# RWKV time mixing: 22 instead of 18 units transposed by the DMA crossbar, the last two loads held so that loads and transposes take turns, slot shifts by ScalarE

## Chip, cores, metric

One core of a Trainium2 chip. The metric is device time of one execution in microseconds (us). Executions of one kernel mostly agree within some tenths; an execution counts as slow when it is over 1.5% above the fastest of its kernel, and comparisons use fast runs. Kernels sent together ran on one chip, beside fresh runs of the kernel before.

## The reference

```python
x_prev[:, 1:, :] = x[:, :-1, :]                    # x: 16 x 2048 x 256, float32
xv = x * time_mix_v + x_prev * (1 - time_mix_v)    # and xr alike
v = xv @ value_weight                              # 256 x 256
r = xr @ receptance_weight
out = (sigmoid(r) * v) @ output_weight             # the k branch isn't used
```

## The kernel before

The 16 batches are cut into 64 units of 512 rows. Each unit needs x transposed (features on partitions). Then, per unit: `psum_r` (4 matmuls), sigmoid on ScalarE, `psum_v` (4), their product `z_sb` on VectorE, `psum_o` (8), its copy on ScalarE, and a store per two units. The mixing with x_prev is a scaled copy of `xt` (VectorE, GpSimd, ScalarE by turns) plus an add of `xt` one slot further on (VectorE).

The first 46 units are transposed by TensorE, six units ahead, and copied out of PSUM by ScalarE; the last 18 by the DMA crossbar (a DMA that transposes what it moves), issued by the sync queue (SP):

```python
BYDMA = 4 * UB + 2                  # UB = 4 units a batch; 18 units by the crossbar
CROSS = NU - BYDMA - LOOK           # 64 - 18 - 6 = 40: first unit in which TensorE transposes nothing
...
xpool  = tile_pool(name="xpool", bufs=6)     # loaded batches, bf16
xtpool = tile_pool(name="xtpool", bufs=3)    # transposed batches
...
def load(b):                        # float32 in DRAM to bf16: a casting load, so from GpSimd's queue
    return nc.gpsimd.dma_start(out=x_bf[b], in_=rows(b), max_dma_last_dim=8192)

def by_dma(b, lo, hi, after=None):
    op = nc.sync.dma_start_transpose(out=xt[b][:, 1 + lo : 1 + hi]..., in_=x_bf[b][:, lo:hi]...)
    if after is not None:
        tc.add_manual_dep(op.ins, after.ins.name, SYNC, reason="not beside a load")
...
for g in range(NU - 1):
    project(ps_r, g, 0); sigmoid
    if g == CROSS:
        by_dma(B - 5, 1 * UJ, 3 * UJ, last_load)       # half of batch 11, after load 15
    advance(...)                                       # TensorE transposes; load b + 5 at each batch
    for b in range(B - 4, B):                          # batches 12 to 15, whole
        if g == max(UB * (b - 2) - 1, CROSS + 1):
            new_xt(b); by_dma(b, 0, J); shifted = b
    output(g - 2) ...; scale, add, project(ps_v, g, 1), z_sb, scale_pool, add ...
    if shifted is not None and g == max(UB * (shifted - 2), CROSS + 2):
        nc.sync.dma_start(out=xt[shifted][:, 0, :, 1:P], in_=xt[shifted][:, J, :, 0 : P - 1])
```

Each queue works in program order. So SP's queue carries stores, crossbar transposes and slot shifts one behind the other, and GpSimd's carries its products and the loads.

## Time and profile before

| | kernel before |
|---|---|
| time, median of 5 | 204.13 us (203.94 to 207.01) |
| span of the profiled run | 202.7 us |
| psum_r start to psum_r start, TensorE transposing / not | 3.05 / 2.60 us |
| last load lands | 134.3 us |

The interval between two psum_r starts, read off the timeline unit by unit, is the measure: whatever exceeds 2.60 us in the crossbar stage is a stall. The prediction below shows the views. Two lines that it quotes only in prose are needed later. They are the DMA queues in 117 to 127 us of the kernel before (packets, MB, share of 16 engines): loads, then stores.

```profile
q0 software_dynamic: 302, 1.17, 57.8%
q1 hardware_dynamic: 246, 1.88, 46.4%
```

The loads took 5.78 of 10 us for 1.17 MB, so 5.2 us of all engines for one batch (1024 KB as bf16, which the view counts as 1.05 MB); the stores 4.64 us for 1.88 MB, so 2.6 us for a store of two units (1024 KB). The share adds up the times of packets and can pass 1.

### The profile page before, as it was taken

How to read it: one execution, taken by the hardware profiler on the slowest of the kernel's cores; microseconds unless marked ns; L12 is line 12 of the kernel's file. 1: busy time of each engine (PE TensorE's matmuls, PEld its weight loads, DVE VectorE, ACT ScalarE, POOL GpSimd, SP SyncE). 2: the span in 40 equal slices, each digit the busy share in tenths (PEclk: the TensorE clock that was granted, in tenths of full speed). 3: DMA queues.
4: the chain of work that ended last, by engine and by line, in shares of the span. 5: the costliest groups of instructions: out<-in, count | busy, mean ns of one | idle time of the engine just before them, and what ended most of it. 6: DMA issues, size and time to landing. Idle time of an engine off the chain costs nothing.

```text
span 202.7 us, 3923 instructions
## 1 busy us (share of the span) xinstructions
PE 195.4 (96%) x1436; PEld 126.2 (62%) x1436; DVE 187.6 (93%) x301; ACT 179.3 (88%) x198; POOL 83.7 (41%) x109
## 2 busy tenths in 40 slices
PE   8899999999999999999999999999899999999992
PEld 7565676666666666666666666655455566665570
DVE  3799999999999999999999999999999999999952
ACT  2599899999999999999999999998798999999981
POOL 1655443462542545344363542443444444444200
PEclk9999999999999999999999999999999999999999
DMA  5999999999999999999999999999999999899475
GB/s 164 294 159 215 241 276 274 279 282 272 293 318 309 313 318 302 293 308 303 289 301 289 293 309 308 292 308 197 287 174 376 246 352 244 276 409 372 200 304 207
DMA packets 32186, 57.00 MB, mean 281 GB/s; under 512 B 20772, under 2 KB 22056, under 8 KB 29096
## 3 DMA queue, kind: packets, MB, share of 16 engines
q1 hardware_dynamic: 27216, 40.50, 59.3%
q0 software_dynamic: 4800, 16.12, 40.1%
q8 instruction: 11, 0.18, 0.3%
q10 hardware_dynamic: 152, 0.13, 0.2%
q14 instruction: 7, 0.06, 0.1%
HBM read 34.34 MB, written 33.55 MB: 335 GB/s over the span
## 4 chain that ended last, share of the span: by engine, by line
PE 80%; DVE 7%; ACT 5%; issue 4%; DMA 2%; SPq 0%; DVEq 0%; ACTq 0%
PE psum_v L279 24%; PE psum_r L279 22%; PE psum_o L303 22%; PE ps_t L200 9%; DVE z_sb L548 3%; DMA w_f<-n_receptance_weight_dram 2%; ACT s_sb L513 2%; DVE mix L271 2%; ACT o_sb L335 2%; DVE mix L249 1%; PE psum_r L293 1%; PE ps_t L303 1%; ACT mix L491 1%; ACT xt L216 0%; PE ps_t L279 0%
## 5 line engine op out<-in xcount | busy, mean ns | idle before, releaser
L259 POOL TENSOR_SCALAR mix<-xt,c_sb 128x1024 bf16<-128x1024 bf16 (+1 forms) x55 | 61.4, 1116 | 92.3 <-DVE mix L271 80.8
L548 DVE TENSOR_TENSOR z_sb<-s_sb,psum_v 128x1024 bf16<-128x1024 bf16 x63 | 76.6, 1215 | 3.4 <-PE psum_v L279 1.7
L271 DVE TENSOR_TENSOR mix<-mix,xt 128x1024 bf16<-128x1024 bf16 x112 | 77.4, 699 | 1.7
L279 PEld LDWEIGHTS <-w_bf 128*128 128x128 bf16 x516 | 48.6, 98 | 39.5 <-issue 2.1
L513 ACT ACTIVATE s_sb<-psum_r 128x1024 bf16<-128x1024 f32 x63 | 65.0, 1032 | 6.2 <-PE psum_r L279 5.9
L335 ACT COPY o_sb<-psum_o 128x1024 f32<-128x1024 f32 x60 | 61.1, 1018 | 7.0 <-PE psum_o L303 7.0
L279 PE MATMUL psum_v<-mix,w_bf 128*128 128x512 bf16 (+1 forms) x256 | 65.3, 377 | 1.2 <-DVE z_sb L548 1.1
L279 PE MATMUL psum_r<-mix,w_bf 128*128 128x512 bf16 (+1 forms) x252 | 64.2, 377 | 0.3 <-ACT s_sb L513 0.3
L303 PE MATMUL psum_o<-wo_bf,z_sb 128*128 128x256 bf16 x494 | 64.4, 273 | 0.1
L303 PEld LDWEIGHTS <-z_sb 128*128 128x128 bf16 x512 | 49.9, 98 | 20.1 <-DVE z_sb L364 0.8
L216 ACT COPY xt<-ps_t 128x1024 bf16<-128x1024 bf16 x38 | 38.7, 1029 | 0.0
L200 PEld LDWEIGHTS <-x_bf 128*128 128x128 bf16 x344 | 22.4, 98 | 9.5 <-DMA x_bf<-in_x_dram 0.5
L200 PE MATMUL ps_t<-ident,x_bf 128*128 128x128 bf16 x344 | 25.7, 219 | 0.0
L249 DVE TENSOR_SCALAR mix<-xt,c_sb 128x1024 bf16<-128x1024 bf16 (+1 forms) x50 | 23.4, 475 | 0.0
L491 ACT ACTIVATE mix<-xt,c_sb 128x1024 bf16<-128x1024 bf16 x11 | 12.8, 1160 | 0.0
L109 POOL DMA_DIRECT2D x_bf<-in_x_dram x14 | 10.5, 752 | 0.0
L271 DVE TENSOR_TENSOR mix<-mix,xt_first 128x1024 bf16<-128x1024 bf16 x15 | 10.1, 681 | 0.1
L259 POOL TENSOR_SCALAR mix<-xt_first,c_sb 128x512 bf16<-128x512 bf16 x6 | 4.2, 694 | 8.0 <-DVE xt_first L408 8.0
L249 DVE TENSOR_SCALAR mix<-xt_first,c_sb 128x512 bf16<-128x512 bf16 x22 | 6.7, 351 | 0.2
L216 ACT COPY xt_first<-ps_t 128x1024 bf16<-128x1024 bf16 x5 | 5.2, 1035 | 0.0
L144 PE MATMUL ps_t<-zeros 128*128 128x128 bf16 x31 | 3.1, 282 | 1.0 <-DVE zeros L87 1.0
L209 ACT CAST xt_first<-ps_t 128x512 bf16<-128x512 f32 x4 | 2.1, 588 | 1.6 <-PE ps_t L200 1.6
(63 smaller groups left out, 46.9 us busy)
## 6 DMA issues: line engine op xcount, KB each, us to landing
out_dram<-o_sb SPq DMA_DIRECT2D x28, 1024.0 KB, 9.7
x_bf<-in_x_dram POOLq DMA_DIRECT2D x14, 1024.0 KB, 27.6
out_dram<-o_sb SPq DMA_DIRECT2D x4, 512.0 KB, 3.6
out_dram<-o_sb SPq DMA_DIRECT2D x6, 256.0 KB, 2.1
x_bf<-in_x_dram POOLq DMA_DIRECT2D x5, 256.0 KB, 6.9
o_sb<-in_x_dram SPq DMA_DIRECT2D x2, 512.0 KB, 5.3
o_sb<-in_x_dram SPq DMA_DIRECT2D x2, 256.0 KB, 2.9
out_dram<-o_sb SPq DMA_DIRECT2D x3, 128.0 KB, 2.0
```

The lines of the kernel that those rows point to most:

```text
L109: return nc.gpsimd.dma_start(out=x_bf[b], in_=rows(b), max_dma_last_dim=8192)
L200: nc.tensor.transpose(out=ps[:, jj], in_=src[:, jj, ko * P : (ko + 1) * P], identity=idn)
L216: nc.scalar.copy(out=xt[b][:, j0 : j0 + UJ], in_=ps)
L249: nc.vector.tensor_scalar(out=mixed(piece)[:, :, ko], in0=xt[b][:, slots(piece), ko], scalar1=c_sb[:, m, ko : ko + 1], scalar2=None, op0=A ...
L259: op = nc.gpsimd.tensor_scalar(out=mixed(piece)[:, :, 1], in0=xt[b][:, slots(piece), 1], scalar1=c_sb[:, m, 1:2], scalar2=1.0, op0=ALU.mul ...
L271: return nc.vector.tensor_tensor(out=mixed(piece), in0=mixed(piece), in1=xt[b][:, slots(piece, 1)], op=ALU.add)
L279: nc.tensor.matmul(out=ps[:, mo, :], lhsT=w_bf[:, m, ko, mo * P : (mo + 1) * P], rhs=mixed((b, m, e * TU + lo, e * TU + hi))[:, :, ko], st ...
L303: nc.tensor.matmul(out=ps[:, slot, :], lhsT=z[:, ko, jj * P : (jj + 1) * P], rhs=wo_bf[:, ko, :], start=(ko == 0), stop=(ko == KO - 1),)
L335: nc.scalar.copy(out=o_sb[b][:, j0 : j0 + UJ, :], in_=ps)
L491: nc.scalar.activation(out=mixed(piece)[:, :, ko], in_=xt[b][:, slots(piece), ko], func=ACT.Copy, scale=c_sb[:, m, ko : ko + 1],)
L513: nc.scalar.activation(out=s_sb, in_=ps_r, func=ACT.Sigmoid)
L548: nc.vector.tensor_tensor(out=z_sb, in0=s_sb, in1=ps_v, op=ALU.mult)
```

## The change

Intent: four more units without TensorE transposes and ScalarE evictions. As these begin while loads are still due, loads 14 and 15 are held: load 14 waits for the transpose of batch 11, the transposes of batch 12 wait for load 14, and so on. The slot shift becomes a small ScalarE copy.

```diff
-    BYDMA = 4 * UB + 2
+    BYDMA = 5 * UB + 2
     CROSS = NU - BYDMA - LOOK                        # now 36
+    CROSS_AT = {B - 6: CROSS - 2, B - 5: CROSS - 1, B - 4: CROSS + 4, B - 3: CROSS + 6, B - 2: CROSS + 12, B - 1: CROSS + 15}
+    HELD_AT = {B - 2: CROSS, B - 1: CROSS + 8}
+    AFTER = {B - 6: B - 3, B - 4: B - 2, B - 2: B - 1}
...  # in advance()
-                last_load = load(b + 5)
+                if b + 5 not in HELD_AT:
+                    loads[b + 5] = load(b + 5)
...  # in the loop over units
+        for b, at in CROSS_AT.items():
+            if g == at:
+                ...
+                crossed = by_dma(b, lo, hi, loads[AFTER[b]] if b in AFTER else None)
+            if g == UB * (b - 1) and b > B - 6:
+                nc.scalar.copy(out=xt[b][:, 0, :, 1:P], in_=xt[b][:, J, :, 0 : P - 1])
...  # at the end of a unit
-        if shifted is not None and ...:
-            nc.sync.dma_start(...)
+        for b, at in HELD_AT.items():
+            if g == at:
+                loads[b] = load(b)
+                tc.add_manual_dep(loads[b].ins, crossed.ins.name, SYNC, reason="not beside a transpose")
```

More of the change, by code (lines that the diff above doesn't have):

```diff
@@ L186, in by_dma @@
             tc.add_manual_dep(op.ins, after.ins.name, SYNC, reason="not beside a load")
+        return op
     def transposes(i):
@@ L412 @@
     tnext = 1
-    last_load = None
+    loads = {}
+    crossed = None
     def advance(limit):
-        nonlocal tnext, last_load
+        nonlocal tnext
         while tnext <= min(limit, NU - 1):
@@ L498 @@
     z_prev2 = z_prev = None
-    shifted = None
     for g in range(NU - 1):
@@ L513 @@
         nc.scalar.activation(out=s_sb, in_=ps_r, func=ACT.Sigmoid)
-        if g == CROSS:
-            by_dma(B - 5, 1 * UJ, 3 * UJ, last_load)
         advance(START_T[g] if g < len(START_T) else g + LOOK)
-        for b in range(B - 4, B):
-            if g == max(UB * (b - 2) - 1, CROSS + 1):
-                new_xt(b)
-                by_dma(b, 0, J)
-                shifted = b
+        for b, at in CROSS_AT.items():
+            if g == at:
+                whole = b > B - 6
+                if whole:
+                    new_xt(b)
+                lo, hi = (0, J) if whole else (UJ, 3 * UJ)
+                crossed = by_dma(b, lo, hi, loads[AFTER[b]] if b in AFTER else None)
+            if g == UB * (b - 1) and b > B - 6:
+                nc.scalar.copy(out=xt[b][:, 0, :, 1:P], in_=xt[b][:, J, :, 0 : P - 1])
         if LATE_O < g < NU - 2:
@@ L556 @@
             advance(4)
-        if shifted is not None and g == max(UB * (shifted - 2), CROSS + 2):
-            nc.sync.dma_start(
-                out=xt[shifted][:, 0, :, 1:P], in_=xt[shifted][:, J, :, 0 : P - 1]
-            )
+        for b, at in HELD_AT.items():
+            if g == at:
+                loads[b] = load(b)
+                tc.add_manual_dep(loads[b].ins, crossed.ins.name, SYNC, reason="not beside a transpose")
         z_prev2, z_prev = z_prev, z_sb
```

## The prediction

> **What bounds the kernel now.** I read first the busy shares, then the groups, then the busy time by stretch, then the timeline and the sync queue's waits around the place that the change edits (130 to 180 us), last the DMA queues there. The page gives the roles:
>
> ```profile
> PE 195.4 (96%) x1436; PEld 126.2 (62%) x1436; DVE 187.6 (93%) x301; ACT 179.3 (88%) x198; POOL 83.7 (41%) x109
> L216 ACT COPY xt<-ps_t 128x1024 bf16<-128x1024 bf16 x38 | 38.7, 1029 | 0.0
> L200 PE MATMUL ps_t<-ident,x_bf 128*128 128x128 bf16 x344 | 25.7, 219 | 0.0
> ```
>
> TensorE is the bound (96%), and 344 of its matmuls only transpose. The busy time by stretch shows two regimes. The columns after the stretch and its length are the engines' busy us with counts, then granted clock, DMA share and GB/s:
>
> ```profile
> 80.00:100.00 20.00, 20.00 (x158) 13.23 (x156) 18.93 (x27) 18.58 (x21) 8.79 (x9) 1.00 1.04 300
> 140.00:150.00 10.00, 9.36 (x57) 5.37 (x56) 10.00 (x13) 8.42 (x9) 4.32 (x6) 1.00 1.10 216
> 150.00:160.00 10.00, 9.79 (x62) 5.74 (x60) 10.00 (x14) 9.09 (x10) 4.46 (x5) 1.00 1.10 327
> 160.00:170.00 10.00, 10.00 (x63) 6.05 (x62) 9.97 (x15) 9.18 (x11) 4.52 (x5) 1.00 1.05 302
> ```
>
> With transposes on TensorE a unit takes 3.05 us (in the timeline psum_r starts at 123.85 and 126.90); without them 2.60 us (157.24, 159.84, 162.44). In the second regime VectorE is full too: 9.97 of 10 us. So from there a delay of VectorE is a delay of the kernel. The DMA share is about 1 in all four rows, the second point to keep. Counting psum_r starts back from the end (unit 63 at 194.78), unit 40 starts at 132.99; the crossbar starts there:
>
> ```profile
> 139.40 1.46 POOL L259 TENSOR_SCALAR mix<-xt,c_sb 128x1024 bf16<-128x1024 bf16 x1 [2.93 <-DVE z_sb L548]
> 139.79 1.35 DVE L249 TENSOR_SCALAR mix<-xt,c_sb 128x1024 bf16<-128x1024 bf16 x1
> 142.92 1.02 PE L279 MATMUL psum_v<-mix,w_bf 128*128 128x512 bf16 x4 [0.64 <-DVE z_sb L548]
> 150.38 1.21 DVE L271 TENSOR_TENSOR mix<-mix,xt 128x1024 bf16<-128x1024 bf16 x1
> ```
>
> The first transposes, issued at 134.44, land 4.8 us later, at 139.2; GpSimd's product at 139.40 waited for them, ran beside VectorE's product (1.35 us in place of 0.48) and TensorE lost time. Between psum_r starts, units 43, 46 and 47 take 3.40, 2.67 and 2.99 us in place of 2.60: **1.26 us of stalls** in the whole late part.
>
> **The DMA side.** A load's time from issue to landing, for the loads issued at 91.07, 103.25 and 115.44 (batches 13, 14, 15), each from the DMA view of a window on that issue:
>
> ```profile
> x_bf<-in_x_dram POOLq DMA_DIRECT2D x1, 1024.0 KB, 26.1
> x_bf<-in_x_dram POOLq DMA_DIRECT2D x1, 1024.0 KB, 22.5
> x_bf<-in_x_dram POOLq DMA_DIRECT2D x1, 1024.0 KB, 18.9
> ```
>
> So they land at 117.2, 125.8 and 134.3, one per 8.6 us, though one is issued per 12.2: a queue works itself off until 134. The sync queue then works in order:
>
> ```profile
> SPq L181 <- DMA x_bf<-in_x_dram: 2.8, 1, 2.8
> SPq L558 <- DMA xt<-x_bf: 5.8, 4, 2.1
> 165.79 8.15 SPq L181 DMA_TRANSPOSE xt<-x_bf  x1
> ```
>
> A whole batch's transpose holds this queue 5.1 to 8.2 us and lands 7.3 to 10.1 us after its issue; the two at 155.01 and 165.79, with stores just ahead of them, took 9.1 and 10.1.
>
> **What the Trainium skill says.** (1) "DMA: Bandwidth & Descriptors", "Anatomy of one DMA — SWDGE (gpsimd) path": a semaphore wait for a DMA is served by the issuing sequencer before dispatch. The trace agrees: the sync queue itself stood 2.8 us for the last load. (2) The same page, "Latency and other measured facts", gives 261 GB/s for one non-contiguous DMA transpose and about 350-400 for contiguous. The trace is slower: 217 GB/s where only a transpose moves, 1 MB in 4.8 us. (3) The same page, "Issuing engines are not separate DMA queues": all queues share the 16 engines. In 117 to 127 us the load queue took 57.8% of them and the sync queue 46.4%: full. (4) "SBUF — State Buffer", "Who interferes with whom": a VectorE operation with two SBUF inputs, or in a two-port mode, excludes a GpSimd operation that reads SBUF. The trace agrees: 0.68 us adds take 1.21 at 150.38, beside GpSimd at 149.94.
>
> **The change, part by part.** Here CROSS goes from 40 to 36 and units 42 to 45 leave TensorE.
>
> *Removed.* 4 units of transposes: 4 x (3.05 - 2.60) = **-1.8 us** on the path. ScalarE loses four 1.03 us evictions, beside TensorE, free. If the first crossbar data come well ahead of their use, the 1.26 us of stalls go as well. Best case: -3.06, 204.13 to 201.1 us.
>
> *Added on ScalarE.* Five slot copies of 128x254. The trace has 0.37 us for a 128x256 ScalarE copy. ScalarE waits 0.41 us in each pair of late units, but the PSUM buffers turn over with only about 0.2 to 0.3 us to spare, so I charge 0.06 each: **+0.3 us**, if the data have landed. They replace four DMAs of 2.8 to 4.6 us.
>
> *Moved: the held loads.* Load 14 is issued at the end of unit 36 by GpSimd's queue and waits for batch 11's transpose; load 15 at the end of unit 44 and waits for batch 13's. That GpSimd must stand and wait is the step I trust most. Without stalls psum_r would start at about 123.0 (unit 37), 125.6 (38), then every 2.6.
> - Batch 10's half waits for load 13 at 117.2, keeps the sync queue 2.9 us, lands near 122; its first use is unit 37's GpSimd product (3.1 us after psum_r, 126.1): in time.
> - A store, then batch 11's transpose at 120.9, landing some 8.2 us later: 129. GpSimd should have begun unit 37's product at 126.1; it begins after the wait and 0.75 us of issue, near 129.8, and is done at 131. VectorE wants it after unit 38's z, at about 129.8: 1.2 us, and then the next product runs beside an add. **+1.5 us.**
> - Load 14 shares the engines with two stores, so it lands near 138 (the alone rate, 1 MB in 4.8 us at 218 GB/s early on, plus 4.8 us of two stores at 437 GB/s). Batch 12's transpose stands before it in the sync queue, lands 145; ScalarE's copy in unit 44 wants it at about 144.8: **+0.5.**
> - Batch 13, behind a store: about 152. Load 15 goes then. GpSimd's product of unit 45 is wanted near 149 and comes near 153.3: VectorE loses **+2.0.**
> - Load 15 lands near 162, batch 14's transpose at 169.5; ScalarE's copy in unit 52 wants it near 167.5: **+1.5.** Batch 15 (177) is about in time.
>
> Sum with my middle durations: -3.06 + 0.3 + 5.5 = +2.7, 206.9 us. With 1 us less in each of the seven DMA steps, the stalls nearly go, except 1 us: 202.4.
>
> **The rivals.** *A: the turns fit.* 201.1 to 202.5. For it: the offsets (+4, +6, +8, +12, +15) look chosen from a trace; a load takes 8.6 us, four units 10.4; and no load then halves a transpose's rate. Against it: unit 36 is only one unit after the transposes that its load awaits. *B: the chain load, transpose, transpose, load, transpose becomes the bound,* through GpSimd's and ScalarE's waits, 204 to 208.5. For it: the DMA is full from start to unit 56 already, and the change adds 4 units, some 5 us of engine time at 4.8 us a batch; VectorE has no slack to make a stall good. *C: nothing of the gain but no chain,* the first stall alone (1.5 to 2.5): 202.5 to 204. I give A 0.3, B 0.5, C 0.2.
>
> **Range and chances.** The middle of these is **205.0 us**; A's good end gives the low limit 201.3, B's bad end, with a chain 1.5 us longer, the high one 208.6. Faster by over 2% needs 200.1, under the best case: 0.03. Slower by over 2% needs 208.2: 0.15. Within 2%: 0.82.
>
> **What would show it.** Right: 312 transposing matmuls instead of 344; 2.60 us units from unit 36; GpSimd's queue waiting for a transpose at the two held loads, 3 to 5 us each; VectorE's adds waiting for GpSimd after it; ScalarE waiting in a slot copy. Wrong: batch 11 landing before 126, load 14 under 7 us from issue, or GpSimd busy as before at units 37 and 45; then A holds. The sum fails downwards if DMA steps run faster alone than I took from the shared ones, and upwards if the waits also hold back stores until ScalarE finds no output buffer.

## The result

| | before | after |
|---|---|---|
| median of 5 | 204.13 us | 217.69 us (215.37 to 219.17) |
| fast runs | | 215.37, 216.02, 217.69 |
| ratio of fast runs | | 1.0601 (1.0548 to 1.0654) |
| profiled span, mean granted clock | 202.7 us, 1.00 | 217.2 us, 0.968 (a slow run) |

Ratios here are the mean time of one kernel's fast runs over that of the other's of the same rounds, so not quite the ratio of the medians. The change is 6% slower; 217.69 lies outside 201.3 to 208.6. The profile of the changed kernel fell in a slow execution; its fast runs are 1.2 to 3.6 us shorter than it. What follows rests on events that fast profiles of its variants repeat.

The page of the changed kernel, its busy shares and its transposing matmuls:

```profile
PE 200.4 (92%) x1404; PEld 126.6 (58%) x1404; DVE 187.6 (86%) x298; ACT 179.8 (83%) x201; POOL 83.0 (38%) x109
L204 PE MATMUL ps_t<-ident,x_bf 128*128 128x128 bf16 x312 | 23.3, 219 | 0.0
```

Work went out as planned (312 instead of 344) and the span grew all the same: VectorE has the same 187.6 us in 86% of the span. So it is waiting. Where, the busy time by stretch tells (columns as in the prediction; 0.83 and 0.70 are the granted TensorE clock):

```profile
130.00:140.00 10.00, 7.36 (x37) 3.88 (x35) 6.81 (x9) 5.87 (x7) 5.25 (x6) 0.83 0.97 244
...
150.00:160.00 10.00, 7.29 (x44) 4.19 (x43) 6.12 (x9) 8.68 (x10) 2.76 (x4) 1.00 1.07 320
160.00:170.00 10.00, 8.78 (x45) 5.05 (x46) 8.63 (x11) 6.13 (x7) 4.01 (x5) 0.83 1.02 260
170.00:180.00 10.00, 6.93 (x41) 3.82 (x39) 8.12 (x12) 6.00 (x8) 3.40 (x4) 0.96 0.77 179
180.00:190.00 10.00, 9.66 (x44) 5.22 (x44) 5.76 (x8) 7.46 (x9) 2.23 (x2) 0.70 1.10 311
```

Until 121 us both kernels run alike. From unit 36 the 2.60 us units come as intended, then four stalls (psum_r interval beyond 2.60, both units where two follow on each other): units 39 and 40: 4.3 us; unit 45: 1.75; units 47 and 48: 4.5; units 53 and 54: 6.4. With some tenths elsewhere, 17.6 us. Against that stand 1.8 us of gain and the 1.26 us of old stalls, gone: 17.6 - 3.06 = 14.5, which is the difference of the two spans, 217.2 - 202.7.

The chain behind the stalls is plain in the sync queue's timeline (start, length, what) and in the landing times of the two held loads, issued at 130.22 and 157.60:

```profile
120.66 7.34 SPq L184 DMA_TRANSPOSE xt<-x_bf  x1
...
142.37 4.82 SPq L184 DMA_TRANSPOSE xt<-x_bf  x1
...
147.99 7.06 SPq L184 DMA_TRANSPOSE xt<-x_bf  x1
...
172.26 4.83 SPq L184 DMA_TRANSPOSE xt<-x_bf  x1
```

```profile
x_bf<-in_x_dram POOLq DMA_DIRECT2D x1, 1024.0 KB, 12.0
x_bf<-in_x_dram POOLq DMA_DIRECT2D x1, 1024.0 KB, 14.5
```

Batch 11's transpose starts at 120.66; load 14 goes out at 130.22 and lands at 142.2; batch 12 follows at 142.37, batch 13 at 147.99 (landing 9.1 us later); load 15 at 157.60 to 172.1; batch 14 at 172.26, landing at 179. The timeline of the other engines at the first held load, and at ScalarE's two waiting slot copies:

```profile
130.22 0.75 POOL L112 DMA_DIRECT2D x_bf<-in_x_dram  x1 [5.75 <-DVE z_sb L555]
...
131.02 2.21 POOL L263 TENSOR_SCALAR mix<-xt,c_sb 128x1024 bf16<-128x1024 bf16 x2
132.18 2.20 DVE L275 TENSOR_TENSOR mix<-mix,xt 128x1024 bf16<-128x1024 bf16 x2 [2.13 <-POOL mix L263]
133.84 1.04 PE L283 MATMUL psum_r<-mix,w_bf 128*128 128x512 bf16 x4 [2.64 <-DVE mix L275]
...
136.24 1.91 PE L283 MATMUL psum_v<-mix,w_bf 128*128 128x512 bf16 x4
```

```profile
149.71 0.40 ACT L528 COPY xt<-xt 128x254 bf16<-128x254 bf16 x1 [1.54 <-DMA xt<-x_bf]
...
178.97 0.40 ACT L528 COPY xt<-xt 128x254 bf16<-128x254 bf16 x1 [3.58 <-DMA xt<-x_bf]
```

GpSimd stands 5.75 us before the load. (The engine named as releaser, VectorE's z_sb, had long been done; the load waits for the transpose.) VectorE then waits 2.13 us for GpSimd and TensorE 2.64 us for VectorE. And one thing was not foreseen: four matmuls that took 1.03 us now take 1.91. The granted clock is read from short stretches of the busy-time view:

```profile
131.30:134.70 3.40, 0.86 (x4) 0.40 (x5) 2.52 (x3) 0.38 (x1) 2.08 (x3) 1.00 0.85 154
134.70:138.10 3.40, 3.40 (x14) 1.86 (x13) 2.50 (x4) 2.93 (x4) 1.82 (x3) 0.53 1.04 235
138.10:141.50 3.40, 3.40 (x21) 1.85 (x20) 2.93 (x4) 2.37 (x3) 0.96 (x2) 0.97 0.92 283
```

After 3.4 us in which TensorE worked only 0.86, its clock is halved for the next 3.4, and 14 matmuls pass where 21 do afterwards. The same happens at 162.0 to 165.4 and, for twice as long, at 179.1 to 185.9. The length of the wait doesn't decide it alone. In a fast run of a variant below ("A load with the DMA to itself") TensorE waits 2.54 us, with the same 0.86 us of work in 3.4, and the clock stays whole, as it does after a wait of 3.38 us there:

```profile
130.40:133.80 3.40, 0.86 (x5) 0.21 (x3) 1.84 (x2) 1.17 (x2) 2.56 (x3) 1.00 0.69 93
133.80:137.20 3.40, 3.40 (x22) 1.96 (x20) 3.40 (x6) 2.51 (x4) 1.29 (x3) 1.00 1.06 213
```

### The profile page after: what moved, and what is told of

It is laid out like the page before. It is cut to its first block, busy times and chain, and to the rows that moved or that the text cites. A ratio compares the mean times of both kernels' runs of the same rounds, so it can differ in the third digit from the quotient of the medians.

```text
span 217.2 us, 3851 instructions
## 1 busy us (share of the span) xinstructions
PE 200.4 (92%) x1404; PEld 126.6 (58%) x1404; DVE 187.6 (86%) x298; ACT 179.8 (83%) x201; POOL 83.0 (38%) x109
## 4 chain that ended last, share of the span: by engine, by line
PE 64%; DMA 14%; DVE 9%; ACT 5%; issue 4%; POOL 2%; SPq 1%; POOLq 0%; DVEq 0%; ACTq 0%
PE psum_v L283 19%; PE psum_o L307 18%; PE psum_r L283 18%; DMA xt<-x_bf 11%; PE ps_t L204 7%; DVE mix L275 5%; DMA o_sb<-in_x_dram 3%; DVE z_sb L555 2%; ACT o_sb L339 2%; POOL mix L263 2%; ACT s_sb L518 1%; DVE mix L253 1%; ACT mix L497 1%; POOL x_bf L112 1%; PE ps_t L307 0%
## 5 line engine op out<-in xcount | busy, mean ns | idle before, releaser
L275 DVE TENSOR_TENSOR mix<-mix,xt 128x1024 bf16<-128x1024 bf16 x112 | 78.7, 710 | 10.5 <-ACT mix L497 4.5
L307 PE MATMUL psum_o<-wo_bf,z_sb 128*128 128x256 bf16 x494 | 67.0, 280 | 4.9 <-ACT o_sb L339 4.8
L283 PE MATMUL psum_r<-mix,w_bf 128*128 128x512 bf16 (+1 forms) x252 | 65.4, 382 | 5.8 <-DVE mix L275 5.4
L283 PE MATMUL psum_v<-mix,w_bf 128*128 128x512 bf16 (+1 forms) x256 | 68.0, 389 | 0.3 <-DVE z_sb L555 0.2
L220 ACT COPY xt<-ps_t 128x1024 bf16<-128x1024 bf16 x34 | 34.6, 1030 | 0.0
L204 PEld LDWEIGHTS <-x_bf 128*128 128x128 bf16 x312 | 20.4, 98 | 8.3
L204 PE MATMUL ps_t<-ident,x_bf 128*128 128x128 bf16 x312 | 23.3, 219 | 0.0
L253 DVE TENSOR_SCALAR mix<-xt,c_sb 128x1024 bf16<-128x1024 bf16 (+1 forms) x48 | 21.5, 457 | 0.0
L497 ACT ACTIVATE mix<-xt,c_sb 128x1024 bf16<-128x1024 bf16 x13 | 15.0, 1154 | 0.0
L528 ACT COPY xt<-xt 128x254 bf16<-128x254 bf16 x5 | 2.0, 397 | 5.1 <-DMA xt<-x_bf 5.1
```

Of the source, the lines that this page charges most:

```text
L204: nc.tensor.transpose(out=ps[:, jj], in_=src[:, jj, ko * P : (ko + 1) * P], identity=idn)
L220: nc.scalar.copy(out=xt[b][:, j0 : j0 + UJ], in_=ps)
L253: nc.vector.tensor_scalar(out=mixed(piece)[:, :, ko], in0=xt[b][:, slots(piece), ko], scalar1=c_sb[:, m, ko : ko + 1], scalar2=None, op0=A ...
L275: return nc.vector.tensor_tensor(out=mixed(piece), in0=mixed(piece), in1=xt[b][:, slots(piece, 1)], op=ALU.add)
L283: nc.tensor.matmul(out=ps[:, mo, :], lhsT=w_bf[:, m, ko, mo * P : (mo + 1) * P], rhs=mixed((b, m, e * TU + lo, e * TU + hi))[:, :, ko], st ...
L307: nc.tensor.matmul(out=ps[:, slot, :], lhsT=z[:, ko, jj * P : (jj + 1) * P], rhs=wo_bf[:, ko, :], start=(ko == 0), stop=(ko == KO - 1),)
```

## The experiments

At this point my theory was the prediction's: GpSimd's stands and ScalarE's waits are the loss, made by the holding. The rivals: the ScalarE copies are dear; 22 units are too many for the DMA however the loads are placed; the halved clock is a cause of its own.

### Shifts alone

The kernel before, with only the shift moved to ScalarE (for batches 12 to 15, in unit 4(b-1)).

```diff
+            if g == UB * (b - 1):
+                nc.scalar.copy(out=xt[b][:, 0, :, 1:P], in_=xt[b][:, J, :, 0 : P - 1])
-        if shifted is not None and ...: nc.sync.dma_start(...)
```

> The kernel before with one part of the change alone: the slot shifts of the last four batches by ScalarE copies instead of DMAs; 18 crossbar units and the loads as before. My theory (the held loads' chain of waits makes the loss): ScalarE's copies find their data landed, cost about 0.1 us each, and the sync queue no longer stands for its own transposes, so 203.3 to 204.6 us. Rival (the ScalarE copies themselves are dear, because ScalarE has little slack in the late units): each of the four costs 1 to 3 us, 207 us or more.

204.27, 205.39 and 206.75 us in three runs, 1.009 (1.003 to 1.015); the profiled execution was an outlier of 417.58 us in which everything took twice as long, of no use. So it was run again.

> The shift-only kernel again, because its profile fell in an execution of twice the length. Unheld, it took 1.009 of the kernel before. Theory (each ScalarE copy costs what the 22-unit kernel without held loads shows in its even stretch, 0.14 us per two units): four copies make 0.6 us, so 204.4 to 205.2, each copy with its data landed. Rival (a copy waits for its transpose): a wait of ScalarE for a transpose of 0.5 us or more in the profile.

204.69 us, ratio 1.001 (0.998 to 1.004). In its profile each copy lengthens two following units by 0.14 us together (2.70 and 2.64 in place of 2.60 twice), and the 0.4 us stall at units 46 and 47 is gone. The two even out. The two rounds lie at and somewhat above the upper end of the first theory (203.3 to 204.6), far from the rival's 207: the copies are not the loss.

### 22 units, loads not held

```diff
-    HELD_AT = {B - 2: CROSS, B - 1: CROSS + 8}
+    HELD_AT = {}
```

> The changed kernel with its 22 crossbar units, its issue points and its ScalarE shifts, but the last two loads not held: they are issued where the kernel before issues them. My theory: the chain load, transpose, transpose, load, transpose is broken at its root, GpSimd never stands for a transpose; the transposes of batches 10 and 11 run beside the loads of 14 and 15 and land later than they did (batch 11 near 133), which still serves; 201 to 204 us. Rival (the DMA engines cannot take 22 units at all in this stretch, however the loads are placed): 208 us or more, with ScalarE or VectorE waiting for transposes.

208.96 us, ratio 1.026 (1.022 to 1.029). My expectation missed, and the rival's number (208 or more) came: slower than before, but some 8 us faster than the change. The profile fell in its one slow run (213.36 us); no trace of the fast ones (208.52 to 209.35) exists, so the sizes that follow are those of a slow run. Its timeline:

```profile
115.59 15.89 SPq L184 DMA_TRANSPOSE xt<-x_bf  x1
...
137.35 0.49 DVE L253 TENSOR_SCALAR mix<-xt,c_sb 128x1024 bf16<-128x1024 bf16 x1 [7.90 <-DMA xt<-x_bf]
...
139.62 1.86 PE L283 MATMUL psum_v<-mix,w_bf 128*128 128x512 bf16 x4 [7.76 <-DVE z_sb L555]
```

Half a batch, which keeps the sync queue 3.1 us in the changed kernel, keeps it 15.9 us beside loads 14 and 15, and VectorE's product that waits for it starts at 137.35. The loads land at 123.9 and 134.5, against 125.8 and 134.3 before, so here it is the transpose that comes late. But the two together move little: 107 GB/s in 124 to 134 us, where the kernel before moves 326 with a load and stores. After that one stall (11.3 and 3.6 us for units 39 and 40) every unit up to the 60th takes 2.6 to 2.8 us. So both of my first assumptions fell: unheld, batch 11 does not "still serve", and the holding is not the whole loss.

### Held, without GpSimd's wait

The two loads at their new places, without the wait for the transpose (it orders traffic, not data).

> The changed kernel with the two held loads at the same places in GpSimd's program, but without their wait for the transposes (a wait that orders traffic, not data). My theory: the stalls after GpSimd's two stands (2.8 + 1.5 us at units 39 and 40, 2.9 + 1.6 us at units 47 and 48, clock loss included) go, and the chain gets some 6 us shorter at each load; what stays is part of ScalarE's wait for batch 14: 203 to 207 us. Rival (GpSimd's stand is harmless because transposes beside loads are as bad): 213 us or more.

220.14 us median: one fast run of 212.49, three slow ones near 220 (so no ratio). My 203 to 207 missed; the fast run is near the rival's 213. The profile is one of the slow runs. In it the stalls after GpSimd's stands are gone, but load 15 went out at 146.73, one us after batch 13's transpose was issued, and transpose and load took this long to land:

```profile
xt<-x_bf SPq DMA_TRANSPOSE x1, 23.4
x_bf<-in_x_dram POOLq DMA_DIRECT2D x1, 1024.0 KB, 21.2
```

The transpose landed at 169.1, ScalarE's copy waited 11.9 us for it, and one psum_r interval is 16.15 us. Here the load was late as well, and the rate fell to 92 GB/s (152 to 167 us). So the reason that the change gives for holding the loads is a real one, as far as two slow runs can show it.

### Empty matmuls where TensorE stood

40 matmuls of zeros before units 40 and 48, 20 in unit 45, 50 in unit 53, as `warm_up(n)`.

> The changed kernel with 150 empty matmuls (zeros, into a spare PSUM tile) put just before the four matmul groups that stood and waited: 40 before units 40 and 48, 20 in unit 45, 50 in unit 53. They take only time in which TensorE stood. Theory: of the 14.5 us lost about 6 are the halved TensorE clock that followed three of the stalls (13.65 us at 0.5 in the profiled run); kept busy, TensorE keeps its clock, 210 to 213 us and a mean clock of 0.995 or more. Rival (the halved clock is an effect beside the path, the waits set the time alone): unchanged, 215 to 219 us.

216.56 us, ratio 1.063 (1.059 to 1.067), the profile in a fast run with mean clock 0.989. My expectation missed; the number is the rival's, and the fast runs of the change have the same mean, 216.4. The clock was kept where the filling met the stall: units 39 and 40 took 4.84 and 2.60 us instead of 5.41 and 4.11. But unit 45 then took 8.30 instead of 4.35. Its 20 empty matmuls were over before TensorE stood, and the clock was halved there (0.57 in 153 to 156 us), which it had not been in the changed kernel. The sync queue of this kernel:

```profile
142.86 5.16 SPq L184 DMA_TRANSPOSE xt<-x_bf  x1
...
172.75 4.81 SPq L184 DMA_TRANSPOSE xt<-x_bf  x1
```

Batches 12 and 14 go out within 0.5 us of when they do in the changed kernel. ScalarE's copy in unit 44 waited 4.30 us instead of 1.54, and its copy in unit 52 started at 179.49 instead of 178.97. So the stalls are not terms that add up: the chain of DMAs sets the time at which unit 52's data exist, and a gain before that is lost there. As one halving was left, the clock's own share isn't settled to the last us.

### A load with the DMA to itself

The stores of units 35 and 37 wait for load 14, those of 43 and 45 for load 15.

```diff
+    STORE_AFTER = {35: B - 2, 37: B - 2, 43: B - 1, 45: B - 1}
+            if g in STORE_AFTER:
+                tc.add_manual_dep(op.ins, loads[STORE_AFTER[g]].ins.name, SYNC, reason="load first")
```

> The changed kernel, with the stores of units 35 and 37 made to wait for load 14 and those of units 43 and 45 for load 15, so that a held load has the DMA engines to itself. Theory (the chain held load, transposes, held load, transpose sets the time, and a load takes 12.0 and 14.5 us because two or three stores go beside it): a load lands 7 to 8 us after issue, the chain is some 10 us shorter, 207 to 211 us. Rival (GpSimd's stands and the halved clock set the time, not the loads' length): at least 214 us.

219.09 us, 1.073 (1.068 to 1.078). My 207 to 211 missed; the number is the rival's, though the next run refutes the rival's first cause. Both loads landed as expected, but the transpose behind them did not profit:

```profile
x_bf<-in_x_dram POOLq DMA_DIRECT2D x1, 1024.0 KB, 8.1
```

```profile
139.14 9.50 SPq L185 DMA_TRANSPOSE xt<-x_bf  x1
```

8.1 us instead of 12.0 and 14.5: the two or three stores beside a held load are what lengthens it. But the put-off stores then stand ahead of batch 12's transpose, which lands 10.9 us after its issue instead of 7.3: at 150.0, where the change had 149.7. The time moved, it did not vanish, so a long load alone is not the loss. Nor was the DMA full all the time: while the first load ran alone (130.0 to 138.1 us), its queue took 73.4% of the engines and nothing else to speak of moved. Taking turns leaves engines idle. In 130 to 180 us the changed kernel moved 238 GB/s (share 0.94), the kernel before 282 (1.07).

### The held loads later in GpSimd's program

```diff
-    HELD_AT = {B - 2: CROSS, B - 1: CROSS + 8}
+    HELD_AT = {B - 2: CROSS + 2, B - 1: CROSS + 12}
```

(and batch 14's transpose in unit 49 instead of 48).

> The changed kernel with the held loads two and four units later in GpSimd's program (ends of units 38 and 48), when the transposes that they await have nearly landed, so that GpSimd hardly stands; batch 14's transpose is issued one unit later, in unit 49. Theory of the chain: the loads go out at the same times as before (130 and 157 to 158 us), batch 14 lands at the same 179, and what GpSimd no longer loses ScalarE waits in its slot copy: 214 to 218 us. Rival (my prediction's first cause, GpSimd's stand itself): the stalls at units 39 to 40 and 47 to 48, 8.8 us with the clock, are simply gained: 207 to 210 us.

219.28 us, 1.075 (1.071 to 1.079), a little over my 214 to 218. No stand of GpSimd for these loads is left, and the stalls after them are gone. ScalarE's copies in its profile (a fast run) read:

```profile
148.85 0.40 ACT L528 COPY xt<-xt 128x254 bf16<-128x254 bf16 x1 [5.11 <-DMA xt<-x_bf]
...
178.78 0.40 ACT L528 COPY xt<-xt 128x254 bf16<-128x254 bf16 x1 [6.54 <-DMA xt<-x_bf]
```

The copies start at 148.85 and 178.78, in the changed kernel at 149.71 and 178.97. Against my expectation load 15 went out 6 us later (163.86), but with next to no store beside it (0.03 MB) it took 8.1 us and landed at the same 172.0. The rival, GpSimd's stand as the cause, is refuted; the chain's landing times and ScalarE's longer waits came as the theory had them.

### 22 units without the last two loads

Wrong result: batches 14 and 15 are not loaded, their units transpose batches 12 and 13 again. As nothing is held, the transpose of batch 12 waits for load 13 instead of 14. Everything else is the changed kernel.

```diff
+    HELD_AT = {}
+    AFTER = {B - 6: B - 3, B - 4: B - 3}
...  # in advance()
+                if b + 5 >= B - 2:
+                    x_bf[b + 5] = x_bf[b + 3]
```

> Wrong result on purpose: the changed kernel with its 22 crossbar units and issue points, but without the loads of batches 14 and 15 at all (their units transpose batches 12 and 13 a second time), so nothing is held and no load is in flight after 117 us. Theory (in the crossbar stage stores and transposes fill the DMA engines nearly to the brim, and the two loads are what does not fit): all stalls go, 22 units give their 1.8 us and the early stalls' 1.3 less 0.7 for five ScalarE copies, 201.2 to 203.0. Rival (22 transposes are too many beside the stores even without loads): 205 or more.

202.20 us, ratio 0.991 (0.987 to 0.995), as the theory had it. The busy time by stretch:

```profile
130.00:140.00 10.00, 10.00 (x62) 5.76 (x60) 9.67 (x14) 9.38 (x11) 4.14 (x6) 1.00 0.99 270
140.00:150.00 10.00, 10.00 (x61) 5.80 (x60) 9.99 (x15) 9.18 (x12) 3.90 (x5) 1.00 1.06 286
150.00:160.00 10.00, 10.00 (x64) 5.95 (x62) 9.81 (x14) 9.34 (x11) 4.42 (x5) 1.00 1.07 303
```

TensorE never waits in these 30 us, and up to unit 60 no unit is longer than 2.77 us. 22 crossbar units, five ScalarE copies and these issue points are fine; the two loads are what doesn't fit. The DMA share is still 0.99 to 1.07 here (1.15 and 0.74 in the two stretches of 10 us that follow). The run takes away the loads' traffic and the waits for them together, so it doesn't tell which of the two costs more.

### 20 and 16 units, loads as before

```diff
-    BYDMA = 4 * UB + 2
+    BYDMA = 5 * UB          # or 4 * UB; batch 11 whole by the crossbar, or not at all
...  # and its issue and slot shift to match
```

> The kernel before with 20 crossbar units instead of 18: batch 11 whole, loads not held, the transposes only after the last load, its slot shift by VectorE, the others as before. Theory (the last load lands at 134 whatever is done, and the crossbar stage cannot begin before it): batch 11's transpose is issued at 134 and lands near 142, wanted near 136; a stall of 4 to 6 us, with the halved clock after it 1 to 2 more, against 0.9 us gained: 207 to 211. Rival (two units more would have fitted; only the holding was wrong): 203 to 205.

> The kernel before with 16 crossbar units instead of 18: batch 11 wholly by TensorE, batch 12 first by the crossbar, one unit later than before. Theory: two units of TensorE transposes cost 0.9 us and the 0.8 us stall of the first transpose goes; 203.6 to 205.0, so that 18 is the edge of what fits. Rival (the crossbar is a loss altogether): below 203.4.

20 units: 208.31 and 205.97 us in its fast runs, 209.31 and 209.67 in the slow ones. The transposes of batch 11 started at 133.88, right after the last load, and two units take 7.33 and 3.27 us, a stall of 5.4. 16 units: 205.92 us, 1.009 (1.005 to 1.013), somewhat above what I expected: its first whole-batch transpose is wanted about as soon as it lands, too, so the stalls did not all go. The row of unheld kernels, 16, 18, 20 and 22 units, is thus 1.009, 1, about 1.013 (my division of the fast runs' mean, 207.1, by the median of before beside them, 204.4 us) and 1.026. Eighteen is the best of the four.

### Two tries at a faster kernel

The store of unit 37 behind the first transpose; then the same with ScalarE's shifts, each one unit later than in the change.

> The kernel before with one move: the store of unit 37 is issued behind the first crossbar transpose instead of before it, so that load 15 and that transpose go ahead of 1 MB of store. Theory (the first transpose lands about 1 us too late and costs 0.8 us): it lands 1 us earlier, the 0.8 us stall at unit 43 goes, 203.0 to 203.9 where the kernel before takes 204.1. Rival (the store only moves into the way of batch 12's transpose): no gain, 204.0 to 205.0.

> The kernel before with the store of unit 37 behind the first transpose and the slot shifts by ScalarE, each one unit later than the change has them. Theory: the stall at unit 43 (0.8) goes by the first, the waits for slot DMAs (0.4 and the new one at unit 50, 1.3) by the second, against 0.6 us for four copies: 202.6 to 203.8 where the kernel before takes 204.1. Rival (the moved store comes back as another wait): 204.5 or more.

205.94 us, 1.0075 (1.004 to 1.011), and 204.46 us, 1.0025 (0.998 to 1.007). In the first the 0.8 us stall at unit 43 is gone as planned, but unit 47 takes 3.92 us: the moved store stands in the way of the next transpose. The second takes most of that back and gains nothing. No correct version beat the kernel before.

## Why the prediction was wrong, step by step

- **Right: the gain.** Units of 2.60 us came from unit 36; the run without the last loads shows 202.2, inside the range that I gave rival A (201.1 to 202.5).
- **Right: the waits and their places; wrong: what they cost.** GpSimd stood before the held loads, VectorE waited for it after unit 38, ScalarE waited in its copies in units 44 and 52. Batch 11's transpose was put at 120.9 and came at 120.66. But GpSimd's stand, the step that I trusted most, is not what costs: without it (held later) the time was no better, 1.075.
- **Right in kind, half in size: the copies.** I charged 0.3 us for five; 0.14 each were measured, 0.7 together. They cost much only when their data are late.
- **Wrong: the terms "Load 14 ... lands near 138" and "Load 15 lands near 162".** I gave the loads some 9 and 10 us; they took 12.0 and 14.5, and landed at 142.2 and 172.1. I had counted two stores at 437 GB/s beside the first and added the load alone. Alone a load takes 8.1 (stores put off), not 4.8: I took the rate of a queue of loads for the time of one from issue to landing. So batch 14's data came at 179.0 instead of 169.5. Set beside the 11 us between 206.9, my sum, and 217.7, these 9.5 are most of the miss; the fast profile of the later-held run repeats the 12.0 and the landings at 172 and 179. A shorter load alone would not have saved it: cut to 8.1, it left the time at 1.073, as the stores put off for it held up the next transpose.
- **Missing: the clock.** My sum has no term for it. Three times in the profiled run the clock was halved after a stall, for 13.6 us in all. But the filled kernel shows that this term is not to be added either: what it gave back at units 39 and 40 was waited away at unit 45. It explains part of the stalls at units 39, 40, 47 and 48, and may explain part of the spread of the change's runs (0.992 in the fastest, 0.967 in the slowest); with most of it filled, the mean was the same.
- **Wrong in form: a sum of stalls.** I added +1.5, +0.5, +2.0 and +1.5. With one chain of DMAs setting the pace, as these runs suggest, the total is when the chain's last link lands, less when it is wanted, and the single stalls only say where that was paid. Later held loads and filled matmuls moved the payment, not the total.
- **Wrong in weight: rival B's bound.** I wrote that the DMA was full until unit 56 and that the change adds 5 us of it, and then gave half the chance to lesser outcomes. (Weighted by these chances the rivals' middles give 204.3, not the 205.0 that I named.) An estimate from the trace of before would have warned: a batch in the crossbar stage lasts 4 x 2.60 = 10.4 us; its two stores take 2 x 2.6 = 5.2 us of the engines, its transposes 4.8 (1024 KB at 217 GB/s): 10.0 us. That leaves 0.4 us per batch, and a load needs 5.2. In the earlier stage a batch lasts 12.2 us, and stores and load take 5.2 + 5.2. So by this estimate loads fit in the first stage only, and the second can begin when the last load has landed, at 134 us, which is where the kernel before begins it. The run without the loads (no stall) and the row 16, 18, 20, 22 agree with this. By the ratios, 0.991 without the two loads, 1.026 with them unheld and 1.060 with them held, about half of the loss is the loads beside 22 units and about half is the holding.
- **Wrong: what a mix would cost.** Under rival A I wrote that a load beside it "halves a transpose's rate". Measured, in the two slow runs that were profiled, the sync queue was held five times as long for half a batch (15.9 against 3.1 us), and a batch landed after 23.4 us instead of 9.1. In the fast runs, 4 to 7 us shorter, it was probably less; no trace shows it.

What stays open: why a transpose and a casting load together move only some 100 GB/s, and how much of this a fast run shows; how much of the loss is the engines' time and how much the order of the one sync queue, which carries stores and transposes (stores on another queue, or the last loads issued earlier into more buffers, were not tried); and why the kernel with the moved store runs 1 to 2 us above its own profiled execution (204.47) in later rounds.

## What to carry to other kernels

When work is moved from an engine to the DMA queues, add up, for one period of the stage that it moves to, the engine time of every transfer there: if the sum with the new work is over the period, expect a loss. No order of issue that was tried here saved it, and taking turns added the landing time of each turn. Where a chain of dependent transfers sets the pace, don't add the stalls that it causes; follow the chain to its last link and compare that one landing with the time at which it is wanted. And before blaming a wait, remove it alone and look whether the next one grows by as much.

## What the Trainium skill lacked or had wrong

- "DMA: Bandwidth & Descriptors", "Rules for kernel authors", says that a transpose next to ordinary DMAs "needs nothing". That is on correctness, and the results here were correct; but the page lacks the cost. Beside GpSimd's casting loads (slow runs) half a batch held its queue 15.9 us instead of 3.1, a whole one landed after 23.4 us instead of 9.1, the load beside it after 21.2, and both together moved 92 to 107 GB/s.
- The same page's 261 GB/s and 350-400 GB/s for a DMA transpose ("Latency and other measured facts"), and "TRN2 transpose DMAs are as fast as regular DMAs" in "Advanced Engine Details and Errata", "X-Bar Transpose (TRN2)": the traces have 216 to 218 GB/s where only a transpose moves (143.9 to 147.2 us of the changed kernel), against 415 for stores (183 to 186 us of the kernel before).
- "TensorE: Matmul & The Clock Gate", "Part 1: The HAM clock gate (the "warmup" mystery)", has the clock halved after at least one idle window of about 3.4 us, and lacks how much work such a window may hold. Here the clock was halved, for 3.4 us, after 3.4 us with 0.86 us of matmuls in it and a wait of 2.64 us; but after waits of 2.54 and 3.38 us in another run it was not.
- No page gives the time of a load that casts: 1024 KB of bf16 took 8.1 us from issue to landing with no store beside it, 12.0 with two and 14.5 with two to three.
